# Up projection of a gated decoder layer: the order of the high-part and low-part products within four contraction tiles

## The chip, the cores and the metric

One NeuronCore of a Trainium2 chip runs the whole kernel, in one launch. The metric is the device time of one execution in microseconds (us); before the change it is 1492.02 us, the median of three runs (1491.55 to 1495.32).

## The reference, cut to what matters

The kernel computes one decoder layer on 256 tokens with a model width of 2048, in float32. The part that the change touches is the MLP:

```
hm = rmsnorm(x, g_mlp)                                   # x: (1, 256, 2048)
x  = x + square(relu(hm @ w_up)) @ w_down                # w_up: 2048 x 8192, w_down: 8192 x 2048
```

Before it stand a combined input projection, two attention mixers, their gates and an output projection; behind it a gated per-layer embedding. Nothing of these is touched.

## The kernel before, in words

**How a float32 product is made.** TensorE's operands are in a format that keeps fewer bits than float32 (fp32r). So each operand is split in two: a high part, which is the value converted to fp32r, and a low part, which is what the conversion dropped. `split` (lines 80 to 83) does it: ScalarE (ACT) writes the high part (line 82), VectorE (DVE) subtracts it from the source and writes the low part (line 83). A product then consists of high times high, low times high and high times low.

**The up projection** (`up_units`, from line 516). Weights are the stationary operand. For each of the 16 contraction tiles kt (128 rows of w_up, 128 columns of it) the activations stand in SBUF as `h2[kt]`, a high and a low block of 256 tokens side by side. Line 526 multiplies the high part of the weights, `wh`, with both blocks at once: 512 columns into one PSUM bank `ps`. Line 527 multiplies the low part, `wl`, with the high block alone: 256 columns, added into the left half of the same bank. So each kt has one matmul of 512 columns and one of 256, and each of the two has its own weight load (LDWEIGHTS). After 16 tiles ScalarE copies the right half out, VectorE adds the left half (lines 532 and 533), and after two such products `hidden` squares and splits the result for the down projection.

**Weights.** A DMA of 1 MB brings 16 tiles of one product (`load`, line 91). `split_weights` splits them in pieces of 8 contraction tiles: one `wh` and one `wl` of 128x1024 for each piece. All such pieces of the kernel share three buffers for `wh` and three for `wl`, so ScalarE can only write a new `wh` when the last matmul that reads the oldest one is done.

**Slabs.** The MLP runs over eight slabs of 1024 hidden columns. The up projection of slab 0 runs alone (its PSUM tag is `s`). After that the up projection of slab s+1 is woven together with the down projection of slab s: half of it by `fast_units` (a scheme with fewer products but sums of weight quarters on VectorE, lines 546 to 560), half by `plain_units` (lines 628 to 630). `together` interleaves the streams, which are Python generators; each `yield` is a point where another stream may go on. `up_units` yields after 8 contraction tiles and after 16. `advance` moves a clock that the program keeps while it emits instructions; work put off with `later` is emitted when that clock has passed its due time.

**What sets the order.** The order in which the code emits instructions is a priority, not yet the order on an engine. The tile framework plans each engine's order when the program is built: an engine whose next instruction is not ready by the plan's own clock is given another one that is. On the chip each engine then runs its list in that fixed order, with semaphores for the dependences between engines. Matmuls into one PSUM bank keep their order among themselves.

Of the kernel before, what the change touches and what calls it, by code (L numbers as in the profile page):

```python
# [17 lines left out]
T = 256  # L18
D = 2048
DT = D // P  # L20
# [39 lines left out]
def layer_kernel(ctx: ExitStack, tc: tile.TileContext, xt, xm, pt, gains, qkg, cst,  # L60
                 wa, wba, wbb, wo, wup, wdn, wpg, wpp, out):
    nc = tc.nc
# [26 lines left out]
    def load(src, nk, cols):  # L89
        raw = wts.tile([P, nk, cols], F32, tag="raw", name="raw")  # L90
        nc.sync.dma_start(raw.rearrange("p k c -> p (k c)"), src)
        return raw

    def split_weights(raw, nk, cols, step=None):

        step = step or 1024 // cols
        parts = []
        for k0 in range(0, nk, step):
            n = min(step, nk - k0)
            wh = wts.tile([P, n, cols], F32R, tag="wh", name="wh")  # L100
            wl = wts.tile([P, n, cols], F32R, tag="wl", name="wl")
            split(wh, wl, raw[:, k0:k0 + n, :])
            parts += [(wh[:, i, :], wl[:, i, :]) for i in range(n)]
        return parts
# [11 lines left out]
    def advance(us):  # L116
        clock[0] += us
        while True:
            due = [e for e in pending if e[0] <= clock[0]]
            if not due:  # L120
                return
            e = min(due, key=lambda e: e[:2])
            pending.remove(e)
            e[2](*e[3])

    def flat(a):
        return a.rearrange("p a t -> p (a t)")

    def group_m(chunks, lhs, load=lambda src: weights(src, 4, 512)):

        ps = [bank("mm") for _ in range(2)]
        last, kt = len(lhs) - 1, 0
        for src in chunks:
            for wh, wl in load(src):
                for tt in range(2):
                    t = slice(tt * P, (tt + 1) * P)
                    nc.tensor.matmul(ps[tt], lhs[kt][:, 0, t], wh, start=kt == 0, stop=False)  # L137
                    nc.tensor.matmul(ps[tt], lhs[kt][:, 0, t], wl, start=False, stop=False)  # L138
                    nc.tensor.matmul(ps[tt], lhs[kt][:, 1, t], wh, start=False, stop=kt == last)  # L139
                kt += 1  # L140
                advance(1.3)
        return ps
# [32 lines left out]
    def new_acts(name, n=DT, pool=None):  # L175
        tiles = [block([P, 4, 2, T], F32R, f"{name}{i}", pool) for i in range(n // 4)]
        return [tiles[k // 4][:, k % 4, :, :] for k in range(n)]
# [100 lines left out]
    for n, (dst, gain) in enumerate(((qT, gq[:, 0, :]), (kT, gq[:, 1, :]))):  # L278
        for g in range(2):
            if rt is None:  # L280
                ps = group_m(range(4), h, first_weights)
                rt = x_norm()
            else:
                ps = group_m([wa[2 * n + g, c] for c in range(4)], h)
# [91 lines left out]
    for n, dst in enumerate((qS, kS)):  # L376
        for g in range(2):
            later(2, dilated_head, 4 * n + 2 * g)
            later(13, dilated_head, 4 * n + 2 * g + 1)
            ps = group_m([wa[6 + 2 * n + g, c] for c in range(4)], h)  # L380
# [20 lines left out]
    for g in range(4):  # L401
        later(2, sb_head, 2 * g)
        later(13, sb_head, 2 * g + 1)
        ps = group_m([wa[12 + g, c] for c in range(4)], h)
        for tt in range(2):
            nc.scalar.activation(ga[tt][:, cols(g)], ps[tt], AF.Copy, scale=rt[:, tt:tt + 1])
    for g in range(4):
        ps = group_m([wba[g, c] for c in range(2)], ya)
# [19 lines left out]
    for g in range(4):  # L428
# [6 lines left out]
        ps = group_m([wbb[g, c] for c in range(2)], yb)  # L435
# [29 lines left out]
    h2 = new_acts("h2_", pool=blk)  # L465
    ss1 = const.tile([P, 2, 4], F32, name="ss1")
    for g in range(4):
        ps = group_m([wo[g, c] for c in range(4)], m)
# [23 lines left out]
    def bank2(tag, bufs=1):  # L492
        return ps2.tile([P, 512], F32, tag=tag, name=f"ps_{tag}", bufs=bufs)
# [3 lines left out]
    def hidden(s, fast):  # L497

        n = 8 if fast else 4
        nc.scalar.activation(s, s, AF.Relu)
        r = mw.tile([P, n, P], F32, tag="hr", name="hr", bufs=1)
        nc.scalar.activation(r[:, 0:4, :].rearrange("p a t -> p (a t)"),
                             s.rearrange("p a t -> p (a t)"), AF.Square)
        if fast:
            a21, a11, a22, a12 = (r[:, i, :] for i in range(4))
            nc.vector.tensor_tensor(r[:, 4, :], a11, a21, op=ALU.subtract)
            nc.vector.tensor_tensor(r[:, 5, :], a21, a22, op=ALU.subtract)
            nc.vector.tensor_tensor(r[:, 6, :], r[:, 5, :], a11, op=ALU.subtract)  # L510
            nc.vector.tensor_tensor(r[:, 7, :], r[:, 6, :], a12, op=ALU.add)
        u = hid.tile([P, 2, n, P], F32R, tag="hid", name="u")
        split(u[:, 0], u[:, 1], r)
        return u
# [3 lines left out]
    def up_units(s, out, tag="mm"):  # L518

        for g in range(4):  # L520
            sums = mw.tile([P, 2, T], F32, tag="hs", name="hs", bufs=2)
            for j in range(2):
                ps = bank2(tag, 4 if tag == "s" else 2)
                parts = split_weights(load(wup[4 * s + g, j], DT, P), DT, P)
                for kt, (wh, wl) in enumerate(parts):
                    nc.tensor.matmul(ps, wh, flat(h2[kt]), start=kt == 0, stop=False)  # L526
                    nc.tensor.matmul(ps[:, :T], wl, h2[kt][:, 0, :], start=False, stop=kt == DT - 1)  # L527
                    advance(0.347)
                    if kt == 7:
                        yield  # L530
                t = mw.tile([P, T], F32, tag="ev", name="ev", bufs=2)
                nc.scalar.activation(t, ps[:, T:], AF.Copy)
                nc.vector.tensor_tensor(sums[:, j, :], ps[:, :T], t, op=ALU.add)
                if j == 1:
                    out.append(hidden(sums, (s, 0) in FAST or (s, 1) in FAST))
                yield
# [157 lines left out]
    for _ in up_units(0, hids[0], "s"):  # L694
        pass
    for s in range(7):
        hids.append([])
        streams = [(0.5, 16, up_units(s + 1, hids[s + 1]))]
        for n in range(2):
            if (s, n) in FAST:  # L700
                streams.append((0.3, 7, fast_units(s, n, hids[s])))
            else:
                streams.append((0.75, 8, plain_units(s, n, hids[s])))
        together(*streams)
# [13 lines left out]
    for g in range(4):  # L718
        ps = [bank2("m", 2) if g % 2 else bank2("s", 4) for _ in range(2)]
        for c in range(4):  # L720
            for i, (wh, wl) in enumerate(weights(wpg[g, c], 4, PIECE)):
                kt = 4 * c + i
# [72 lines left out]
```

## Time and profile before

| | before |
|---|---|
| median of 3 runs | 1492.02 us |
| profiled execution | 1492.93 us |
| its span, first to last instruction | 1491.1 us |
| mean granted TensorE clock | 0.997 |
| TensorE matmuls (PE) | 1470.8 us busy, 6960 instructions |
| TensorE weight loads (PEld) | 1210.2 us busy |
| VectorE (DVE) | 1000.4 us busy |
| ScalarE (ACT) | 840.3 us busy |
| DMA | 279 MB, 187 GB/s on the mean |

A matmul's recorded duration is longer than the distance to the start of the next one, because matmuls are pipelined: the pace of TensorE is read from the starts of successive matmuls. "wh", "wl", "h", "u" and "ps" in a row are the program's names of buffers. A row "out<-in" says what is written and what is read; in brackets stands the idle time of the engine just before the instruction, and what ended it.

### The profile page before, as it was taken

What the parts mean: (1) busy time and instruction counts of PE and PEld (TensorE: products, weight loads), DVE (VectorE), ACT (ScalarE), POOL (GpSimd) and SP (SyncE); (2) the same over time, 40 slices, a digit from 0 to 9 for tenths busy, and PEclk for the clock granted to TensorE, in tenths of its full rate; (3) what the DMA queues carried; (4) which work ended last, traced back from release to release, by engine and by line L of the source; (5) the groups of instructions that cost most, each with busy time, mean ns of one, the idle gap of its engine ahead of it and who ended that gap; (6) DMA issues with size and microseconds to landing.
All of it is one profiled execution on the core that took longest, in us unless ns stands there. A gap on an engine that the chain in (4) does not pass through costs nothing.

```text
span 1491.1 us, 17831 instructions
## 1 busy us (share of the span) xinstructions
PE 1470.8 (99%) x6960; PEld 1210.2 (81%) x6960; DVE 1000.4 (67%) x1209; ACT 840.3 (56%) x1084; POOL 42.4 (3%) x60
## 2 busy tenths in 40 slices
PE   7999999999999999999999999999999999999998
PEld 5888888888888888888787887878888787878886
DVE  5775555456555555556878879788787878765654
ACT  7444555488834444546655656656565655656543
POOL 0442000000000000000000000000000000000000
PEclk9999999999999999999999999999999999999999
DMA  8555544544455555557455464645546465444563
GB/s 330 174 196 193 175 155 159 194 169 170 169 182 190 193 185 186 194 178 302 141 198 198 170 226 140 228 170 191 204 155 239 143 208 191 159 146 154 201 221 111
DMA packets 40549, 279.09 MB, mean 187 GB/s; under 512 B 4624, under 2 KB 5136, under 8 KB 7312
## 3 DMA queue, kind: packets, MB, share of 16 engines
q1 hardware_dynamic: 40320, 277.92, 53.5%
q8 instruction: 54, 0.88, 0.2%
q14 instruction: 31, 0.25, 0.0%
q10 hardware_dynamic: 144, 0.02, 0.0%
HBM read 275.83 MB, written 2.10 MB: 186 GB/s over the span
## 4 chain that ended last, share of the span: by engine, by line
PE 92%; DVE 3%; issue 2%; DMA 1%; ACT 1%; SPq 0%; DVEq 0%; ACTq 0%
PE ps_mm L137 13%; PE ps_mm L139 13%; PE ps_mm L526 13%; PE ps_mm L138 13%; PE ps_mm L527 7%; PE ps_m L629 4%; PE ps_m L630 4%; PE ps_m L628 3%; PE ps_s L548 3%; PE ps_s L546 2%; PE ps_s L550 2%; PE ps_s L526 2%; DVE wl L83 2%; DMA raw<-in_wa 1%; ACT wh L82 1%
## 5 line engine op out<-in xcount | busy, mean ns | idle before, releaser
L83 DVE TENSOR_TENSOR wl<-raw,wh 128x1024 fp32r<-128x1024 f32 (+1 forms) x462 | 563.5, 1228 | 341.3 <-ACT wh L82 337.8
L82 ACT ACTIVATE wh<-raw 128x1024 fp32r<-128x1024 f32 (+1 forms) x462 | 485.3, 1054 | 404.2 <-PE ps_mm L139 222.8
L526 PE MATMUL ps_mm<-h,wh 128*128 128x512 f32 x896 | 321.3, 398 | 0.0
L137 PE MATMUL ps_mm<-wh,h 128*128 128x512 f32 x640 | 255.8, 400 | 5.5 <-ACT wh L82 5.5
L527 PE MATMUL ps_mm<-h,wl 128*128 128x256 f32 x896 | 251.8, 281 | 0.4
L138 PE MATMUL ps_mm<-wl,h 128*128 128x512 f32 x640 | 251.2, 393 | 0.6 <-DVE wl L83 0.5
L139 PE MATMUL ps_mm<-wh,h 128*128 128x512 f32 x640 | 251.0, 392 | 0.0
L526 PEld LDWEIGHTS ps_mm<-h,wh 128*128 128x128 f32 x896 | 168.3, 188 | 40.8 <-ACT wh L82 2.3
L83 DVE TENSOR_TENSOR wl<-quart,wh 128x1024 fp32r<-128x1024 f32 x98 | 120.1, 1225 | 83.3 <-ACT wh L82 83.2
L527 PEld LDWEIGHTS ps_mm<-h,wl 128*128 128x128 f32 x896 | 169.0, 189 | 8.2 <-DVE wl L83 3.2
L82 ACT ACTIVATE wh<-quart 128x1024 fp32r<-128x1024 f32 x98 | 104.0, 1061 | 123.2 <-PE ps_mm L526 87.0
L137 PEld LDWEIGHTS ps_mm<-wh,h 128*128 128x128 f32 x640 | 121.0, 189 | 31.7 <-ACT wh L82 8.1
L138 PEld LDWEIGHTS ps_mm<-wl,h 128*128 128x128 f32 x640 | 121.3, 189 | 26.8 <-DVE wl L83 2.6
L139 PEld LDWEIGHTS ps_mm<-wh,h 128*128 128x128 f32 x640 | 121.0, 189 | 25.8
L629 PE MATMUL ps_m<-wl,u 128*128 128x512 f32 x256 | 101.8, 397 | 4.1 <-DVE wl L83 4.0
L630 PE MATMUL ps_m<-wh,u 128*128 128x512 f32 x256 | 100.0, 391 | 0.0
L628 PE MATMUL ps_m<-wh,u 128*128 128x512 f32 x256 | 97.9, 392 | 1.6 <-DVE xr L448 1.6
L548 PE MATMUL ps_s<-wl,u 128*128 128x512 f32 x196 | 80.2, 409 | 0.0
L546 PE MATMUL ps_s<-wh,u 128*128 128x512 f32 x196 | 78.6, 401 | 0.0
L550 PE MATMUL ps_s<-wh,u 128*128 128x512 f32 x196 | 76.7, 392 | 0.0
L560 DVE TENSOR_TENSOR quart<-quart 128x2048 f32<-128x2048 f32 x28 | 64.1, 2289 | 0.5
L629 PEld LDWEIGHTS ps_m<-wl,u 128*128 128x128 f32 x256 | 48.1, 188 | 18.1 <-DVE wl L83 9.2
(204 smaller groups left out, 1826.0 us busy)
## 6 DMA issues: line engine op xcount, KB each, us to landing
raw<-in_wa SPq DMA_DIRECT2D x79, 1024.0 KB, 4.8
raw<-in_wup SPq DMA_DIRECT2D x64, 1024.0 KB, 4.8
raw<-in_wdn SPq DMA_DIRECT2D x36, 1024.0 KB, 4.8
quart<-in_wdn SPq DMA_DIRECT2D x28, 1024.0 KB, 4.8
raw<-in_wo SPq DMA_DIRECT2D x16, 1024.0 KB, 4.8
raw<-in_wpg SPq DMA_DIRECT2D x16, 1024.0 KB, 4.8
raw<-in_wba SPq DMA_DIRECT2D x8, 1024.0 KB, 4.8
raw<-in_wbb SPq DMA_DIRECT2D x8, 1024.0 KB, 4.8
```

The source lines that it names most:

```text
L82: nc.scalar.activation(hi, src, AF.Copy)
L83: nc.vector.tensor_tensor(lo, src, hi.bitcast(F32), op=ALU.subtract)
L137: nc.tensor.matmul(ps[tt], lhs[kt][:, 0, t], wh, start=kt == 0, stop=False)
L138: nc.tensor.matmul(ps[tt], lhs[kt][:, 0, t], wl, start=False, stop=False)
L139: nc.tensor.matmul(ps[tt], lhs[kt][:, 1, t], wh, start=False, stop=kt == last)
L526: nc.tensor.matmul(ps, wh, flat(h2[kt]), start=kt == 0, stop=False)
L527: nc.tensor.matmul(ps[:, :T], wl, h2[kt][:, 0, :], start=False, stop=kt == DT - 1)
L546: nc.tensor.matmul(ps, f[k][:, 0, a, :], wh, start=start and k == 0, stop=False, skip_group_check=not start)
L548: nc.tensor.matmul(ps, f[k][:, 0, a, :], wl, start=False, stop=False, skip_group_check=not start)
L628: nc.tensor.matmul(ps[tt], u[k][:, 0, a, :], wh, start=i + k == 0, stop=False)
L629: nc.tensor.matmul(ps[tt], u[k][:, 0, a, :], wl, start=False, stop=False)
L630: nc.tensor.matmul(ps[tt], u[k][:, 1, a, :], wh, start=False, stop=last)
```

## The change

Within each four contraction tiles the four 512-column products of the high parts come first, one after the other, and then the four 256-column products of the low parts. The clock that the program keeps moves once per four tiles by four times the step, and the `yield` stays after the eighth tile. The number of matmuls, weight loads and splits stays the same.

```diff
-                for kt, (wh, wl) in enumerate(parts):
-                    nc.tensor.matmul(ps, wh, flat(h2[kt]), start=kt == 0, stop=False)
-                    nc.tensor.matmul(ps[:, :T], wl, h2[kt][:, 0, :], start=False, stop=kt == DT - 1)
-                    advance(0.347)
-                    if kt == 7:
+                for k0 in range(0, DT, 4):
+                    for kt in range(k0, k0 + 4):
+                        nc.tensor.matmul(ps, parts[kt][0], flat(h2[kt]), start=kt == 0, stop=False)
+                    for kt in range(k0, k0 + 4):
+                        nc.tensor.matmul(ps[:, :T], parts[kt][1], h2[kt][:, 0, :], start=False,
+                                         stop=kt == DT - 1)
+                    advance(1.388)
+                    if k0 == 4:
                         yield
```

## Rows read from the trace of the kernel before

**Rows 1.** The page, busy time of each engine over the span.
```profile
PE 1470.8 (99%) x6960; PEld 1210.2 (81%) x6960; DVE 1000.4 (67%) x1209; ACT 840.3 (56%) x1084; POOL 42.4 (3%) x60
```

**Rows 2.** Windows: length, busy us of PE, PEld, DVE, ACT, POOL; clock, DMA.
```profile
894.00:983.00 89.00, 88.46 (x439) 72.25 (x438) 72.46 (x83) 52.41 (x63) 0.00 (x0) 1.00 0.55 189
```

**Rows 3.** Waits of weight loads, 650 to 1345 us: total, times, longest.
```profile
PEld ps_s L548 <- DVE wl L83: 9.4, 34, 0.3
PEld ps_m L629 <- DVE wl L83: 9.2, 14, 1.7
PEld ps_mm L527 <- DVE wl L83: 3.2, 7, 0.5
```

**Rows 4.** Timeline, alternating pairs, slab 0 alone: first and last of 41.
```profile
689.73 0.28 PE L527 MATMUL ps_s<-h,wl 128*128 128x256 f32 x1
...
703.94 0.27 PE L527 MATMUL ps_s<-h,wl 128*128 128x256 f32 x1
```

**Rows 5.** Timeline, alternating pairs in a later slab: from 930.06, 14 pairs.
```profile
930.06 0.40 PE L526 MATMUL ps_mm<-h,wh 128*128 128x512 f32 x1
...
932.53 0.40 PE L526 MATMUL ps_mm<-h,wh 128*128 128x512 f32 x1
932.77 0.28 PE L527 MATMUL ps_mm<-h,wl 128*128 128x256 f32 x1
932.89 0.40 PE L526 MATMUL ps_mm<-h,wh 128*128 128x512 f32 x1
...
935.01 0.40 PE L526 MATMUL ps_mm<-h,wh 128*128 128x512 f32 x1
```

**Rows 6.** Timeline of PE, two 256-column matmuls in a row, then 512-column ones.
```profile
327.91 0.40 PE L361 MATMUL ps_at<-spl,tri_r 128*128 128x512 f32 x1
328.15 0.28 PE L362 MATMUL ps_at<-spl,ones_r 128*128 128x256 f32 x1
328.26 0.28 PE L363 MATMUL ps_at<-spl,tri_r 128*128 128x256 f32 x1
328.38 0.39 PE L137 MATMUL ps_mm<-wh,h 128*128 128x512 f32 x1
...
329.31 0.39 PE L138 MATMUL ps_mm<-wl,h 128*128 128x512 f32 x1
```

**Rows 7.** Timeline of PE, undisturbed 512-column matmuls: first and last, six steps.
```profile
331.14 0.39 PE L137 MATMUL ps_mm<-wh,h 128*128 128x512 f32 x1
...
332.50 0.39 PE L137 MATMUL ps_mm<-wh,h 128*128 128x512 f32 x1
```

**Rows 8.** Timeline around a wait of line 527 for its low part.
```profile
939.33 2.35 DVE L83 TENSOR_TENSOR wl<-raw,wh 128x1024 fp32r<-128x1024 f32 x2
940.14 0.39 PE L526 MATMUL ps_mm<-h,wh 128*128 128x512 f32 x1
940.60 0.39 PE L527 MATMUL ps_mm<-h,wl 128*128 128x256 f32 x1
940.82 0.39 PE L526 MATMUL ps_mm<-h,wh 128*128 128x512 f32 x1
```

**Rows 9.** Timeline, 896 to 903 us: order on PE, loads, and VectorE's chain.
```profile
896.53 0.40 PE L546 MATMUL ps_s<-wh,u 128*128 128x512 f32 x1
896.61 1.06 ACT L82 ACTIVATE wh<-quart 128x1024 fp32r<-128x1024 f32 x1 [0.45 <-PE ps_mm L526]
896.77 0.40 PE L526 MATMUL ps_mm<-h,wh 128*128 128x512 f32 x1
...
897.70 1.23 DVE L83 TENSOR_TENSOR wl<-quart,wh 128x1024 fp32r<-128x1024 f32 x1 [0.23 <-ACT wh L82]
...
898.98 0.19 PEld L548 LDWEIGHTS ps_s<-wl,u 128*128 128x128 f32 x1 [0.28 <-DVE wl L83]
...
899.09 0.19 PEld L550 LDWEIGHTS ps_s<-wh,u 128*128 128x128 f32 x1
...
902.72 0.50 PE L629 MATMUL ps_m<-wl,u 128*128 128x512 f32 x1 [0.47 <-DVE wl L83]
```

## The prediction

> **What bounds the kernel now.** I read the page's busy times first: TensorE's matmuls fill 99% of the span, VectorE 67%, ScalarE 56% [rows 1]. A busy share of 99% doesn't say that TensorE runs at its pace, so the stages come next. In one woven slab of the MLP, 89 us long, matmuls are busy for 88.46 us at a granted clock of 1.00, which is the 2.4 GHz level, and VectorE for 72.46 us [rows 2]. So TensorE sets the time. The clock has nothing to give back here, and the DMA share of 0.55 leaves the transfers in the cover.
>
> Two things are left. One is the distance from one matmul's start to the next. The other is where TensorE stands for an operand. In the MLP its weight loads stood for a low part from VectorE for 9.4 us ahead of line 548, 9.2 us ahead of line 629 and 3.2 us, in 7 waits, ahead of line 527, the line that moves [rows 3].
>
> **What the change removes, adds and moves.** It removes and adds no matmul, load, split or DMA. There are 64 products of 16 contraction tiles, so 1024 pairs in 256 groups of four. What changes is which matmul follows which, when a low part is first needed, and when a buffer is last read.
>
> *The pace of a group.* Before, a group is four alternating pairs. While slab 0 runs alone 41 pairs take 703.94 - 689.73 = 14.21 us, 0.347 us each [rows 4]. In a woven slab 14 pairs take 935.01 - 930.06 = 4.95 us, 0.354 us each [rows 5]. The mean of the two is 0.350 us, so 1.40 us for a group. Undisturbed 512-column matmuls take 1.36 / 6 = 0.227 us each [rows 7]. In proportion to the columns a pair should then take 0.227 + 0.113 = 0.340 us: each alternation costs about 10 ns more than its columns.
>
> The trace has one place where short matmuls stand in a row: two of 256 columns between ones of 512 [rows 6]. A 512-column one and two 256-column ones take 328.38 - 327.91 = 0.47 us, of which 0.235 us falls to the two short ones, 0.1175 us each. The four 512-column ones after them take 329.31 - 328.38 = 0.93 us, not 4 x 0.227 = 0.91: the stream is slowed for some matmuls after a short one, not for one alone. This is just the sequence that the change makes. A new group by these rows is 0.93 + 4 x 0.1175 = 1.40 us, by the starts in the row between 1.39 and 1.41. I take 1.395, which is 5 ns less for a group: 256 x 0.005 = 1.3 us gained, all on the path, since TensorE sets the end.
>
> The bounds of this term are wide, because no row shows four short matmuls in a row. At best the slowing goes: four at 0.227 us and four at the 0.11 us that a load takes (the load after the late one starts at 899.09, the late one at 898.98 [rows 9]), so 1.35 us and 256 x 0.05 = 13 us gained. At worst, with the steps of the slowest pairs throughout (0.24 us from 932.53 to 932.77, 0.12 us from there to 932.89 [rows 5]), a group takes 4 x 0.36 = 1.44 us and 256 x 0.04 = 10 us are lost. A load that hid under nothing in such a run would add 0.11 us to each short matmul, 113 us in all, but rows 6 have two in a row without it. I stay with the row that is nearest, rows 6.
>
> The Trainium skill's page "TensorE: Matmul & The Clock Gate" gives, under "Back-to-back issue gap", columns divided by 2.4 GHz plus 2.5 ns at the warm clock, and under "LDWEIGHTS (loading the stationary operand)" a load time of columns divided by 1.2 GHz. An estimate from these is 215.8 ns and 109.2 ns for the two sizes and 106.7 ns for a load, which just fits under the shorter one, so that the order makes no difference and this term is zero; the sum would be 1488.1 us. The trace has 227 ns where the page has 215.8 and shows the neighbours to matter [rows 5 to 7].
>
> *The low part is needed later.* A piece of eight tiles opens with one high-part matmul, and the low part must be there 0.23 us later. After the change four high-part matmuls open it, so the low part has about 3 x 0.227 = 0.68 us more. Where line 527 waits, 0.46 us pass from the 512-column start to it and 0.22 us from there to the next start, against 0.35 us for an undisturbed pair: 0.33 us, made of the wait and of a load that cannot hide behind a running matmul [rows 8]. The extra 0.68 us covers it. With 7 such waits [rows 3] this is 7 x 0.33 = 2.3 us. If VectorE is later than that, the same wait stands behind the four.
>
> *The high part's buffer comes free earlier.* The last read of a `wh` piece was followed by one 256-column matmul of its group, now by four, so ScalarE's next split can start about 3 x 0.1175 = 0.35 us earlier against TensorE's progress. Where this matters is the longest regular stall. ScalarE starts a split at 896.61 on a high-part matmul's release. VectorE, idle for 0.23 us, starts its subtraction at 897.70 behind it, works through its list in order, and TensorE stands for line 629's low part until 902.72 [rows 9]. An earlier release can take away VectorE's 0.23 us and no more, since then VectorE is busy throughout. One such place in each of 7 woven slabs makes 7 x 0.23 = 1.6 us. Bounds: nothing, if another release comes last, and 7 x 0.47 = 3.3 us, all of TensorE's idle time there. The low part's buffer is released at the group's end as before, and its next writer follows a ScalarE split of 1.06 us [rows 9], which covers that.
>
> *The program's clock.* Work put off comes due at the end of a group instead of a pair, at most 1.04 us later by that clock. What falls due in the up projection lies between the same two yields, and I cost it at nothing. The cover is that VectorE emits nothing else between those points; if it is gone, one VectorE sum of weights stands later, within the range below.
>
> *The sum.* 1.3 + 2.3 + 1.6 = 5.2 us from the profiled execution's 1492.93 us (span 1491.1 us and 1.8 us around it) gives 1487.7 us. The median of the runs is 0.9 us under that execution, so 1486.8 us by the median. What is late next is line 548's low part, 34 waits [rows 3], which nothing here touches.
>
> **The rivals.**
>
> *The waits move and don't go* (no change). VectorE's list is in order and 81% busy in a slab (72.46 / 89 [rows 2]). If TensorE merely reaches the next low part of VectorE's earlier and stands there, the 3.9 us of the second and third terms come back at lines 548 and 629 and the pace alone is left: 1492.0 - 1.3 = 1490.7 us. For it: most of the waits are on VectorE. Against it: ScalarE and VectorE start on releases of TensorE, so they too move forward when TensorE does.
>
> *The plan comes out worse* (slower). The order on TensorE is not that of the code: after the first matmul of line 546 at 896.53 comes an up-projection matmul at 896.77, while the code has line 548 next [rows 9]. The plan fills in where by its own clock a low part isn't ready. Other readiness in the up projection gives another weave in the seven slabs, on VectorE as well. If it puts one more VectorE chain ahead of a low part in each half slab, each stall costs the 0.47 us of idle at line 629 and the 0.11 us of an uncovered load [rows 9]: 14 x 0.58 = 8.1 us. With the pace's gain and without the other two it comes to 1492.0 - 1.3 + 8.1 = 1498.8 us. With the other two terms lost it is worse than no change from 3 such stalls on (1.3 / 0.58). Against it: four matmuls that need no low part make the weave less eager to switch, not more.
>
> *The load sets the pace of a run* (slower). Each load starts when the matmul ahead of it starts, and 0.11 us of it against 0.113 us of columns is close. If the third and fourth short matmul in a run pay half a load each, 0.055 us, a group costs 0.11 us more, and 256 x 0.11 = 28 us make 1515 us. It decides from a mean pace of about 0.121 us in the run, where the 15 ns that a group gains from the waits (3.9 / 256) are used up. Against it: two in a row stay at 0.1175 us [rows 6].
>
> **How the numbers follow.** What a measurement of this kernel can tell from no change is 0.3%, 4.5 us: faster is under 1487.5 us, slower over 1496.5 us. The forecast, 1486.8 us, gets 0.46; its own range is 1482 to 1490 us. Waits that move get 0.38, the worse plan 0.11, the load's pace 0.05. The forecast lies near the edge of 0.3%, so it gives some 0.10 to no change; the better half of the pace's bounds gives the first rival some 0.12 of faster, which leaves faster 0.48, same 0.36, slower 0.16. The range for 8 in 10 reaches from 1480 us, half of the pace's best end with the waits gone, to 1496 us, short of the worse plan's 1498.8, which with the load's case makes up most of what is left out.
>
> **What would show it.** After: the starts of four line-526 matmuls about 0.23 us apart, then four short ones 0.115 to 0.12 us apart; a group of 1.39 to 1.40 us; no waits of the low part's load for VectorE in the up projection; line 629's waits shorter. The pace's term is wrong if the short ones stand over 0.12 us apart or the 512-column ones come down to 0.227 us from the first. The second and third terms are wrong if the totals of lines 548 and 629 grow by what the up projection loses. The forecast is wrong as a whole if the order on TensorE outside the up projection differs and stalls stand in new places.

## The result, and the profile after

The changed kernel takes 1507.21 us (median of four runs, 1506.16 to 1509.08) against 1492.26 us for the kernel before on the same chip (four runs, 1491.55 to 1495.32): a ratio of 1.0098, 95% interval 1.008 to 1.0115. It is 15 us slower, where 1486.8 us was forecast and 1480 to 1496 us given as range. The profiled span is 1505.5 us at a mean granted clock of 0.997, the same clock as before.

The change does what it says, and its pace is the one forecast. This is the timeline of TensorE in slab 0 after: start, duration and, at the end, how many matmuls the row stands for.

```profile
687.78 1.09 PE L527 MATMUL ps_s<-h,wh 128*128 128x512 f32 x4
688.71 0.64 PE L529 MATMUL ps_s<-h,wl 128*128 128x256 f32 x4
...
715.85 1.09 PE L527 MATMUL ps_mm<-h,wh 128*128 128x512 f32 x4
```

From 687.78 to 715.85 lie 20 groups in 28.07 us, 1.403 us each; line 527 is now the high part, line 529 the low part. Yet TensorE is busy for less of the span (98%, [rows 1] had 99%), and the same woven stretch as in [rows 2] shows where: 86.42 us busy and 425 matmuls begun in 89 us, against 88.46 us and 439. The first two fences below are the page after and the windows view, with the columns of [rows 1] and [rows 2]; VectorE's and ScalarE's busy times are the same within 2 us.

```profile
PE 1471.5 (98%) x6960; PEld 1209.3 (80%) x6960; DVE 999.1 (66%) x1209; ACT 838.9 (56%) x1084; POOL 42.4 (3%) x60
```

```profile
894.00:983.00 89.00, 86.42 (x425) 70.22 (x425) 71.02 (x81) 51.31 (x62) 0.00 (x0) 1.00 0.53 181
```

The waits of the weight loads after, from 650 us to 1360 us (total, times, longest), which answer to [rows 3]; the stretch is longer by the time lost in it, and the same holds for all such rows below:

```profile
PEld ps_s L549 <- ACT wh L82: 22.0, 35, 2.0
PEld ps_mm L527 <- ACT wh L82: 13.4, 20, 1.0
PEld ps_s L551 <- DVE wl L83: 5.9, 21, 0.3
PEld ps_m L632 <- DVE wl L83: 5.7, 8, 1.3
```

The kernel before had these waits for high parts, which [rows 3] doesn't show (lines 546 and 526 there are 549 and 527 now):

```profile
PEld ps_s L546 <- ACT wh L82: 3.7, 15, 0.3
PEld ps_mm L526 <- ACT wh L82: 2.3, 7, 0.3
```

Before, TensorE stood mostly for low parts from VectorE. After, it stands for high parts from ScalarE (line 82): 22.0 us in place of 3.7 ahead of line 549, the matmul that opens each tile of the fast half, and 13.4 us in place of 2.3 in the up projection. The waits for low parts (lines 551 and 632, which were 548 and 629) are shorter.

Two sums over the matmuls of 512 and 256 columns from 650 us to the end separate pace from waits. The distance from one start to the next, less 0.4415 ns for each column (226 ns for 512), is an excess. Excesses up to 60 ns are the stream's pace; those above are stalls. Before, pace 17.1 us and stalls 22.3 us; after, 15.9 and 37.9. So the pace gained 1.2 us and the stalls lost 15.6 us, which makes the 14.4 us between the two spans.

**What the plan did.** The order on TensorE changed outside the up projection. Written with P for plain, U for up and F for fast matmuls, a stretch of six of the seven woven slabs reads:

```
before  P8 U1 P5 U15 F1 U1 F6 U3 F5 U28 F7 ...
after   P8 U4 P3 U15 F1 U7 F5 U6 P1 F1 P1 U1 F5 U3 F1 U16 F11 ...
```

Where the plan put in one up matmul in the middle of a plain piece, it now puts in four, and leaves the piece two matmuls before its end. Further on in the same slab `U12 P12 U1 P3` has become `U12 P2 U4 P12`. The timeline from 911 to 926 us shows what follows (PE, ACT and DVE; start, duration, and in brackets the engine's idle time before and what ended it):

```profile
911.92 1.21 PE L527 MATMUL ps_mm<-h,wh 128*128 128x512 f32 x4
...
913.43 0.39 PE L631 MATMUL ps_m<-wh,u 128*128 128x512 f32 x1
...
915.27 1.06 ACT L82 ACTIVATE wh<-quart 128x1024 fp32r<-128x1024 f32 x1 [2.46 <-PE ps_mm L527]
...
919.25 1.06 ACT L82 ACTIVATE wh<-quart 128x1024 fp32r<-128x1024 f32 x1 [2.92 <-PE ps_s L553]
919.98 0.39 PE L632 MATMUL ps_m<-wl,u 128*128 128x512 f32 x1
920.70 0.40 PE L633 MATMUL ps_m<-wh,u 128*128 128x512 f32 x1
921.49 0.42 DVE L536 TENSOR_TENSOR hs<-ps_mm,ev 128x256 f32<-128x256 f32 x1
921.58 0.51 PE L527 MATMUL ps_mm<-h,wh 128*128 128x512 f32 x1 [0.48 <-ACT wh L82]
921.82 2.28 DVE L563 TENSOR_TENSOR quart<-quart 128x2048 f32<-128x2048 f32 x1
...
924.39 1.04 ACT L82 ACTIVATE wh<-quart 128x1024 fp32r<-128x1024 f32 x1
925.49 0.50 PE L549 MATMUL ps_s<-wh,u 128*128 128x512 f32 x1 [1.56 <-ACT wh L82]
```

The last three matmuls of a plain piece begin at 913.43, but two of them only follow at 919.98 and 920.70, so its `wh` buffer, one of three, stays held for 7 us more, while ScalarE stands idle for 2.46 and 2.92 us ahead of its splits. Then VectorE's sum of weight quarters (line 563, 2.28 us) begins only behind `hs` at 921.82, the split of its result at 924.39, and TensorE stands 1.56 us for it at 925.49.

### The profile page after: what moved, and what is told of

Same layout as the page of the kernel before. It is cut to its first block, busy times and chain, and to the rows that moved or that the text cites. A ratio compares the mean times of both kernels' runs of the same rounds, so it can differ in the third digit from the quotient of the medians.

```text
span 1505.5 us, 17817 instructions
## 1 busy us (share of the span) xinstructions
PE 1471.5 (98%) x6960; PEld 1209.3 (80%) x6960; DVE 999.1 (66%) x1209; ACT 838.9 (56%) x1084; POOL 42.4 (3%) x60
## 4 chain that ended last, share of the span: by engine, by line
PE 90%; ACT 4%; issue 2%; DVE 2%; DMA 1%; SPq 0%; DVEq 0%; ACTq 0%
PE ps_mm L137 13%; PE ps_mm L138 13%; PE ps_mm L139 13%; PE ps_mm L527 12%; PE ps_mm L529 6%; PE ps_m L632 4%; PE ps_m L633 4%; PE ps_m L631 3%; ACT wh L82 3%; PE ps_s L549 3%; PE ps_s L551 3%; PE ps_s L553 3%; PE ps_s L527 2%; DMA raw<-in_wa 1%; DVE wl L83 1%
## 5 line engine op out<-in xcount | busy, mean ns | idle before, releaser
L527 PE MATMUL ps_mm<-h,wh 128*128 128x512 f32 x896 | 251.0, 396 | 5.6 <-ACT wh L82 5.6
L527 PEld LDWEIGHTS ps_mm<-h,wh 128*128 128x128 f32 x896 | 156.5, 189 | 36.3 <-ACT wh L82 13.4
L529 PEld LDWEIGHTS ps_mm<-h,wl 128*128 128x128 f32 x896 | 137.2, 188 | 18.6
L529 PE MATMUL ps_mm<-h,wl 128*128 128x256 f32 x896 | 142.3, 281 | 0.0
L549 PEld LDWEIGHTS ps_s<-wh,u 128*128 128x128 f32 x196 | 36.7, 187 | 29.4 <-ACT wh L82 22.0
```

What stands on the lines that cost most here:

```text
L527: nc.tensor.matmul(ps, parts[kt][0], flat(h2[kt]), start=kt == 0, stop=False)
L529: nc.tensor.matmul(ps[:, :T], parts[kt][1], h2[kt][:, 0, :], start=False, stop=kt == DT - 1)
L549: nc.tensor.matmul(ps, f[k][:, 0, a, :], wh, start=start and k == 0, stop=False, skip_group_check=not start)
```

## The experiments

The letters in the expectations: by theory **W** (weave) the planned lists lose the time and the new order of pairs gains it; by **H** (held buffer) it is the two plain matmuls put off; by **S** the sum of quarters stands too late against the first fast product that needs it; by **O** it is the four runnable matmuls that open a piece which turn the plan. In the first three runs "rival O" is another thing, the order of long and short matmuls itself. All kernels ran beside the kernel before, which took 1492.26 to 1492.75 us there.

To hold an engine's list, ordering edges (without a semaphore) go along a written-out list once the layer is emitted. The k-th up matmul of the code takes the k-th place of an up matmul on the list (cut):

```
for engine, places in order.items():       # e4: TensorE's list only
    seq = [...]                            # the engine's instructions in that order
    for a, b in zip(seq, seq[1:]):
        tc.add_manual_dep(b, a.name, info, reason="pin")
```

**1. New order of pairs in the old lists** (TensorE, VectorE and ScalarE held as before the change).

> The changed order within four tiles, but the lists of TensorE, VectorE and ScalarE are held to the places they had before the change: the k-th matmul of the up projection stands in the k-th place that the up projection had in TensorE's old list, and VectorE's and ScalarE's lists are the old ones word for word. Theory W (the time was lost because the plan wove the two streams otherwise): the new waits of lines 527 and 549 for ScalarE are gone, and the time is before less 1.3 us of pace and up to 3.9 us of waits: 1487 to 1492 us. Rival O (the order of four long and four short matmuls itself makes the loss, on the chip): about 1507 us. Rival L (the lists are innocent and the load sets the pace of a run): as O, with short matmuls over 0.121 us apart.

Measured 1482.97 us, ratio 0.9935 (0.9922 to 0.9947): 9.8 us faster than before and 24 us faster than the changed kernel, with the same order inside each group of four. Its pace is 15.7 us and its stalls are 13.5 us, by the sums above: 1.4 and 8.8 us less than before. W holds in direction; the time came 4 us under its range, as more waits went than the 3.9 us that it allowed for. The same place of the slab in this kernel (line 924 ends the plain piece, 373 is the split, 854 the sum, 840 the matmul that opens a fast tile):

```profile
905.52 0.39 PE L924 MATMUL ps_m<-wh,u 128*128 128x512 f32 x1
905.95 1.06 ACT L373 ACTIVATE wh<-quart 128x1024 fp32r<-128x1024 f32 x1 [0.80 <-PE ps_m L924]
...
910.40 2.29 DVE L854 TENSOR_TENSOR quart<-quart 128x2048 f32<-128x2048 f32 x1
...
913.72 1.05 ACT L373 ACTIVATE wh<-quart 128x1024 fp32r<-128x1024 f32 x1
...
916.66 0.40 PE L840 MATMUL ps_s<-wh,u 128*128 128x512 f32 x1
```

The sum is done at 912.69 and its split at 914.77, 1.9 us before the matmul that reads it. In the changed kernel that matmul waited 1.56 us.

**2. The old pairs in the changed kernel's lists.**

> The reverse: the old alternating pairs, with all three lists held to the places that they have after the change. Theory W: the waits of the changed kernel stand again, and the low parts are needed earlier besides: 1506 to 1513 us. Rival O: about 1492 us, as before the change.

Measured 1574.46 us, ratio 1.0551 (1.0531 to 1.0571). The direction is W's; the size was missed by over 60 us. The changed kernel's lists open a piece with four matmuls at a time when its low part isn't there; alternating pairs want it after one. The waits of weight loads (line 818 is the up projection's low part):

```profile
PEld ps_mm L818 <- DVE wl L374: 48.6, 32, 2.9
```

The granted clock also fell: its mean over the span is 0.984, against 0.997 before. Between 720 and 1410 us, where TensorE stands for a low part again and again, up to 2.9 us at a time, stretches of 90 to 125 us have means of 0.95 to 0.99. With the lower level at half the pace (1.2 GHz in place of 2.4) that is worth at most some 22 us (an estimate from these means), so most of the 82 us lost is waits.

**3. Groups of two, planned freely** (`range(0, DT, 2)`, two high and two low products, `advance(0.694)`).

> Two long matmuls, then two short ones, left to the plan. The plan's TensorE list for a slab has the same switches between streams as before, give or take one matmul. Theory W: 1488 to 1494 us. Rival O (the loss grows with the length of the runs): about half of the loss, 1497 to 1502 us.

Measured 1486.66 us, ratio 0.9962 (0.9948 to 0.9975); pace 13.9 us, stalls 19.3. The list reads `P8 U2 P5 U14 F1 U1 F6 U2 F5 U29 F7`, close to that of before. With two instead of four in a row the plan comes out well and the order gains; the time lies 1.3 us under the range.

**4. Only TensorE's list held.**

> As the first run, but TensorE's list alone is held to the old weave; VectorE's and ScalarE's lists are planned anew (97 of VectorE's 1209 places and 47 of ScalarE's 1020 differ from before). If TensorE's weave is what cost the time: 1487 to 1494 us. If the lists of VectorE and ScalarE are what cost it: 1500 us or more.

Measured 1483.24 us, 0.9943 (0.9928 to 0.9959), the same as with all three lists. The order on TensorE is enough: with it held, the other two engines' lists cost nothing when they are planned anew.

**5. The two plain matmuls brought back** into their piece, in the changed kernel's lists (six places).

```
-P8 U4 P3 U15 F1 U7 F5 U6 P1 F1 P1 U1 F5 U3 F1 U16
+P8 U4 P5 U15 F1 U7 F5 U6 F1 U1 F5 U3 F1 U16
```

> The changed kernel with all three lists held as the plan made them, but for two matmuls in each of six slabs: the last two (lines 632 and 633) of a plain down-projection piece, which the plan put off behind 28 matmuls of the up projection, go back in front of them. Theory H (held buffer): the two kept one of the three wh buffers for some 7 us, so ScalarE's next pieces for the fast products came late, and lines 549 and 527 waited. Then most of the 24 us by which the new-weave kernel stands over the old-weave one goes: 1485 to 1493 us. Rival D (displacement): the up projection's longer fills between the fast product's matmuls (7, 6 and 3 in place of 1 and 3) are what sets the fast product's chain late; then the two cost little: 1501 to 1507 us.

Measured 1507.87 us, 1.0102 (1.0087 to 1.0118): nothing regained, just above D's range, and H as the whole cause has fallen. The timeline of this kernel shows the buffer coming free and the next thing late (826 is the copy out of the up product, 827 `hs`):

```profile
913.12 1.06 ACT L373 ACTIVATE wh<-quart 128x1024 fp32r<-128x1024 f32 x1 [1.51 <-PE ps_m L924]
914.52 1.06 ACT L373 ACTIVATE wh<-quart 128x1024 fp32r<-128x1024 f32 x1 [0.34 <-PE ps_mm L818]
...
919.18 0.38 ACT L826 ACTIVATE ev<-ps_mm 128x256 f32<-128x256 f32 x1 [3.60 <-PE ps_mm L820]
919.60 0.42 DVE L827 TENSOR_TENSOR hs<-ps_mm,ev 128x256 f32<-128x256 f32 x1 [2.76 <-ACT ev L826]
919.94 2.28 DVE L854 TENSOR_TENSOR quart<-quart 128x2048 f32<-128x2048 f32 x1
...
924.48 0.50 PE L840 MATMUL ps_s<-wh,u 128*128 128x512 f32 x1 [1.55 <-ACT wh L373]
```

Both splits now start by 914.52. But `hs` stands ahead of the sum on VectorE's list and waits for the up product's end, so VectorE stands idle for 2.76 us and the same wait stands at the fast product, 1.55 us. Over the MLP the waits for the fast half's high parts fell from 22.0 to 17.6 us, and those of the up projection grew from 13.4 to 16.9 us: what was taken away at one place came back at the next.

**6. Only the two matmuls put off**, in the old lists.

```
-P8 U1 P5 U15 F1 U1 F6 U3 F5 U28
+P8 U1 P3 U15 F1 U1 F6 U3 F5 P2 U28
```

> The reverse: the new order of four with the old lists (1483.0 us), but in six slabs the last two matmuls of that plain piece are put off behind the next fast product's first twelve. Nothing else moves. Theory H: ScalarE's split for the fast product waits for a buffer as in the changed kernel, at least 1 us in each of six slabs and what hangs on it: 1490 to 1505 us. Rival D: 1483 to 1485 us.

Measured 1506.43 us, 1.0087 (1.0074 to 1.0101): 23.5 us more than the kernel that it was made from (1482.97). D has fallen as the whole cause too, and the time lies 1.4 us over H's range. So putting off two matmuls alone can cost as much as the change did. ScalarE's splits and the fast tiles stand for each other in turn:

```profile
911.82 1.06 ACT L373 ACTIVATE wh<-quart 128x1024 fp32r<-128x1024 f32 x1 [2.42 <-PE ps_mm L818]
912.93 0.50 PE L840 MATMUL ps_s<-wh,u 128*128 128x512 f32 x1 [0.68 <-ACT wh L373]
...
915.65 1.06 ACT L373 ACTIVATE wh<-quart 128x1024 fp32r<-128x1024 f32 x1 [2.77 <-PE ps_s L844]
916.76 0.50 PE L840 MATMUL ps_s<-wh,u 128*128 128x512 f32 x1 [1.15 <-ACT wh L373]
```

This isn't the price of the held buffer in the changed kernel: here the piece stays open for 10 us (from 909.30 to 919.51), there for 7, with other fills around it, and here VectorE's and ScalarE's lists are those of a weave without the delay. In the changed kernel it is one of two late things. With this one taken away, in the kernel with the two matmuls brought back, the other held the time where it was. No run divides the changed kernel's own loss between the two.

**7. One edge in the changed kernel**: the up product's first low-part matmul (second product of its slab) may not come before the end of the plain piece, which makes the plan finish the piece first (cut; `behind` is an ordering edge without a semaphore).

```
+if g == 0 and j == 1 and kt == 0: low[s] = i.ins       # first low-part matmul
+if i == 0 and j == 0: down[s] = o.ins                  # last matmul of the plain piece
+for s in range(1, 7):
+    tc.add_manual_dep(low[s + 1], down[s].name, behind, reason="finish the piece")
```

> The changed kernel, planned freely but for one ordering edge in each of six slabs: the first low-part matmul of one up product stands behind the last matmul of that plain piece. No list is written out. Theory H: the plan finishes the piece first and the time is near that of the held lists: 1482 to 1488 us. Rival D: 1498 us or more, as the fills stay as the plan likes them.

Measured 1486.57 us, 0.9954 (0.9942 to 0.9967); stalls 17.0 us. Six edges turn the 15 us lost into 6 us gained. The list now reads `P8 U4 P5 U12 F1 U2 F11 U30`: the long fills between the fast matmuls are gone together with the open piece, so this run is a cure but doesn't tell H from D.

**8. The sum behind the following split**, in VectorE's old list, else as the first run: `hr, hr, split, sum, split` for `hr, sum, hr, split, split`.

> The new order of four with the old lists, and in VectorE's list one swap in each of six slabs: the 2.29 us sum of weight quarters goes behind the first of the two low-part splits that follow it. That split is what the plain product's low-part matmul stands for, 0.52 us and 0.11 us of load in each slab. If the sum has slack: 6 x 0.63 = 3.8 us gained, 1479 us. If the sum is needed by the next fast product as late as it comes: 1483 us or up to 1490 us.

Measured 1487.11 us, 0.9959 (0.9947 to 0.9972): 4.1 us more than the first run, within the second range, but not for the reason given there. The waits for the plain low part did shrink, from 7.9 to 3.2 us. The fast tiles don't stand for the sum's split any longer than before (3.4 us in both). What came late is the split of `u`, the squared hidden product, which stands behind on the same lists: line 844, the fast matmul that reads the low part of `u`, waits 6.2 us in 6 waits for VectorE, and line 840 4.0 us for ScalarE's high part, neither of which the first run had. The swap moved the wait.

**9. The first fast matmul later**: as the fifth run, and `U3 F1 U16` becomes `U19 F1`, so that 19 up matmuls cover the sum.

> The changed kernel's held lists with the two plain matmuls back (1507.9 us), and besides in each of six slabs one matmul later: the first of the next fast product (line 549 of the changed kernel) goes behind the 16 up matmuls that followed it. VectorE's and ScalarE's lists stay the changed kernel's. Theory S (too little work between a fast product and the next: sum of quarters 2.3 us and ScalarE's split 1.0 us stand uncovered): the 1.7 us wait of that matmul goes and its 0.1 us of load, less what the up matmuls then wait for: 6 x 1 to 6 x 1.8 us, 1497 to 1502 us; the rest of the loss stays with ScalarE's list, where the up product's evacuation stands in front of the next splits. If the wait only moves to the next matmul: 1506 to 1509 us.

Measured 1501.89 us, 1.0066 (1.0052 to 1.0081): 6.0 us less than without it, at the edge of what S had.

**10. The same TensorE list, the other two engines planned anew.**

> TensorE's list of the run before it, with VectorE's and ScalarE's lists planned anew. If TensorE's weave alone makes the loss, the same time as that run within 3 us. If the order of evacuation, sum and splits on VectorE and ScalarE makes the rest of it: 5 us or more under that run.

Measured 1497.27 us, 1.0033 (1.0021 to 1.0045): another 4.6 us lay in the lists of ScalarE and VectorE, which falls between the two ranges. The remaining 14.3 us to the first run lie in the rest of TensorE's weave. No run divides them, but the traces show where TensorE stands: ahead of the up projection's high parts. First the tenth run (line 820), then the first (line 818):

```profile
PEld ps_mm L820 <- ACT wh L375: 15.8, 20, 2.0
```

```profile
PEld ps_mm L818 <- ACT wh L373: 2.3, 7, 0.3
```

The longest of them, 2.0 us, stand at the other place where the list changed, at the `U4` of `U12 P2 U4 P12`.

**11 and 12. Half of the new order, in the old lists.** A piece of eight tiles has two groups. In one kernel the first group is new (low part needed later, the buffer's last read where it was), in the other the second group is (buffer read last 0.35 us earlier, low part needed as before):

```
+four = [("h", kt) for kt in range(k0, k0 + 4)] + [("l", kt) for kt in range(k0, k0 + 4)]
+if k0 % 8 == 4:      # second kernel: == 0
+    four = [(p, kt) for kt in range(k0, k0 + 4) for p in "hl"]
```

> The old lists again (1483.0 us), but of the two groups in each piece of eight tiles only the first has the new order; the second alternates as before the change. So the low part is needed 0.68 us later, as in the changed kernel, but the high part's buffer is read to the end, as before it. If the later need of the low part makes most of the gain of 9.7 us: 1483 to 1486 us. If the earlier release of the buffer makes it: 1487 to 1491 us.

> The complement: the first group of each piece alternates, the second has the new order. The buffer is released 0.35 us earlier, but the low part is needed as early as before. If the release makes most of the gain: 1483 to 1486 us. If the later need makes it: 1487 to 1491 us.

Measured 1486.76 us with the first group new, 0.9960 (0.9948 to 0.9973), between its two ranges, and 1482.92 us with the second group new, 0.9937 (0.9923 to 0.9951). The earlier release alone gives all that the whole order gives in these lists, and the later need alone gives 6.0 us, so the two are not to be added. Alone, the earlier release takes 9.1 us of stalls away and the later need 4.6. The waits for the low parts of the plain product (line 927) and of the fast one (line 846) show where. First the kernel in which the low part is needed later, then the one with the earlier release:

```profile
PEld ps_m L927 <- DVE wl L374: 12.2, 14, 1.6
PEld ps_s L846 <- DVE wl L374: 7.2, 34, 0.3
```

```profile
PEld ps_m L927 <- DVE wl L374: 7.7, 14, 1.4
PEld ps_s L846 <- DVE wl L374: 3.6, 14, 0.3
```

**13 and 14. The same halves, planned freely.**

> No list is held. Of the two groups in each piece of eight tiles the first alternates as before the change, the second has the new order; the plan is free. Theory O (it is the four high-part matmuls that open a piece and need no low part that make the plan weave otherwise): the weave stays near the old one, the buffer is still released early, and the time is near the held lists': 1482 to 1487 us. Rival R (the earlier release of the buffer is what turns the plan): 1495 us or more.

> The complement, with no list held: the first group of each piece has the new order, the second alternates. Theory O: the plan leaves the plain piece unfinished as in the changed kernel, and the time is 1498 us or more. Rival R: 1485 to 1490 us, as in the held run of the same order.

Measured 1485.24 us with the second group new, 0.9952 (0.9939 to 0.9966), and 1517.15 us with the first group new, 1.016 (1.0146 to 1.0174). Each half gains when the lists are held; planned freely, the one that opens a piece with four high-part products loses 24 us and the other keeps `U1 P5` on the list and gains 7.5 us. O holds. The waits of the losing one, whose list has `U4 P3`, are of the kind of the changed kernel's (line 553 is the first fast product, 531 the up projection):

```profile
PEld ps_s L553 <- ACT wh L82: 20.3, 29, 2.0
PEld ps_mm L531 <- ACT wh L82: 19.9, 20, 1.7
```

**The versions that beat both.** The second group's order alone, without any edges, takes 1485.24 us; with the old TensorE list held the new order takes 1483 us. Groups of two (1486.66 us) and the six edges (1486.57 us) beat both as well.

## Why the prediction was wrong

*The pace* (1.3 us gained) was right in size, 1.2 us in the changed kernel and 1.4 us in the old lists, and in part by luck: the prediction's rows gave 1.40 us for the old group and 1.39 to 1.41 us for the new, and the 5 ns were picked out of that. Both groups are some 6 ns longer than it took them to be. A group was to take 1.395 us and takes 1.401 us by the means of its steps (233.7, 233.9, 231.6 and 228.5 ns for the long ones, 116.3, 119.1, 118.9 and 118.7 ns for the short). The matmuls of 512 columns come down only slowly behind short ones, as [rows 6] had shown. At the time of [rows 4 and 5], 0.347 us and 0.354 us a pair, an old group is 1.39 to 1.42 us; over all pairs without a stall it is 1.406 us.

*The low part needed later* (2.3 us) and *the high part's buffer free earlier* (1.6 us) had the right sign with the old lists, and were undersized: together 8.8 us of stalls went. The third term, the earlier release, is the one that was mis-sized most: 1.6 us forecast, at most 3.3, and 9.1 us alone in the twelfth run. It was bounded by TensorE's idle time ahead of the plain low part in [rows 9], 7 x 0.47 us. But the chain of splits has more waits: line 629's 9.2 us and line 548's 9.4 us [rows 3] stand at 7.9 and 3.8 us in the first run, so the fast product's waits for a low part shrank most, of which the prediction said that nothing here touches them. They shrink with the earlier release alone (to 3.6 us) and hardly with the later need (to 7.2 us).

The first run's waits, with lines 923, 842 and 840 for the plain low part, the fast low part and the fast high part:

```profile
PEld ps_m L923 <- DVE wl L374: 7.9, 14, 1.4
PEld ps_s L842 <- DVE wl L374: 3.8, 14, 0.3
PEld ps_s L840 <- ACT wh L373: 3.4, 14, 0.3
```

*What failed* is the step ahead of the sum: it took every term from the weave of before and costed the change's effect on the plan at nothing, though its text named the mechanism, that TensorE's order isn't the code's [rows 9], and gave as the sign of being wrong as a whole just what came: another order outside the up projection and stalls in new places. The rival "the plan comes out worse" had the right place and went the right way. Its argument against itself, that four matmuls which need no low part make the weave less eager to switch, was the reverse of what happened: they are four runnable matmuls where there was one, and the plan leaves the plain piece sooner and stays away longer (`U4 P3 U15` for `U1 P5 U15`); only the kernel that opens a piece with them, planned freely, loses. Its price, 8.1 us from 14 stalls of 0.58 us, was about half of the 15.6 us of stalls that came, because it took one more VectorE chain for the late thing. The late things were high parts from ScalarE. Of stalls over 0.3 us, measured as above, 20 are new: 7 of 1.72 us ahead of line 549, where a sum of 2.28 us and its split of 1.04 us stand uncovered, and 13 of 0.5 to 1.0 us in the up projection. What the buffer that is held for 7 us adds to them was not divided out. The argument that kept its chance at 0.11 was the wrong one.

*The waits that move* did not decide: in the first run the totals of the plain and the fast low part both shrank. But in the eleventh, where the low part is only needed later, the plain low part's waits grew from 9.2 to 12.2 us while the up projection's 3.2 us went, which is the sign that the prediction gave for it; that kernel's gain comes mostly from the fast half, whose stalls fell from 7.0 to 1.5 us. *The load's pace* was wrong as a rival: the third and fourth short matmul stand 118.9 and 118.7 ns apart, under the 0.121 us from which it was to decide.

*The program's clock* was costed at nothing. The order in which the instructions are emitted on VectorE and ScalarE is the same in both kernels. With the old order and the new step of that clock the plan has the old TensorE list in the woven slabs; that kernel was not run. The thirteenth run has the new step and gains 7.5 us, so the step alone is not what loses.

What stays open: how the changed kernel's loss divides between the held buffer, the uncovered sum and the second changed place of TensorE's list. That the 14.3 us between the tenth run and the first come from that place is read from waits and not tested. How much of the second run's 82 us is the lower clock is known only to be under some 22 us.

## What to carry to other kernels

Where a planner sets the engines' lists, a reorder changes two things: what it does to the pairs, and what it offers the planner as filler elsewhere. Build the lists of both kernels and compare them beyond the edited lines before costing anything; if the other streams move, cost those moves first, above all matmuls that hold the last buffer of a shared pool and sums that an in-order engine has behind a later operand. A reorder that pays with held lists can often be had without them by doing it only where it doesn't add runnable work at a switch: here the closing group of each piece, not the opening one.

## What the runs showed of the hardware

Four matmuls of 256 columns in a row stand 116 to 119 ns apart at a granted clock of 1.00, so their weight loads, 0.11 us each by [rows 9], still hide. Behind a run of short ones the first two 512-column matmuls take 234 ns and the fourth still 228.5 ns, against 227 ns undisturbed [rows 7].

The stalls were dear through what stood behind them in order, not through the work that was moved: two matmuls put off in each of six slabs, 0.45 us of work each time by their undisturbed pace, cost 23.5 us over the woven slabs.
